# A new estimate of TensorE's times in the scheduler of a two-layer diffusion step: the same instructions in another order

## The chip, the cores and the metric

The kernel runs on one core of one Trainium2 chip, in one launch. The metric is the device time of that launch in microseconds (us). A core has TensorE (PE in the profile, with its weight loads as PEld), VectorE (DVE), ScalarE (ACT), GpSimd (POOL) and SyncE (SP), which here only issues transfers. Each engine works through its own instructions in program order, and waits where an operand is not there or a buffer is not free.

## The reference

A hybrid diffusion step of two layers on 1024 latent tokens and 256 context tokens, 1024 features wide, in float32. Layer 0 projects the tokens, runs a recurrence over them in both directions (RWKV-7, 8 heads of 64), runs a short gated convolution beside it, and projects back. Layer 1 is attention with 16 query heads and 4 key heads of 64. Cut to what matters here:

```
def rwkv_scan(S0, r, w, k, v, kk, a, reverse):
    def step(S, inp):
        r_t, w_t, k_t, v_t, kk_t, a_t = inp
        sk = jnp.einsum('bhvk,bhk->bhv', S, kk_t)
        S = (S * w_t[:, :, None, :] - sk[..., None] * (kk_t * a_t)[:, :, None, :]
             + v_t[..., None] * k_t[:, :, None, :])
        return S, jnp.einsum('bhvk,bhk->bhv', S, r_t)
    ...
def rwkv_conv_mixer(h, S0, w_in, ...):
    proj = h @ w_in
    ...
    S_f, y_f = rwkv_scan(S0[:, 0], ..., False)
    S_b, y_b = rwkv_scan(S0[:, 1], ..., True)
    ...
    out = jnp.concatenate([out_a, out_b], axis=-1) @ w_out
def block_attention(q, k, v):
    ...
        s = jnp.einsum('bqhgd,bhkd->bhgqk', qblk, k).astype(f32) * scale
        p = jax.nn.softmax(s, axis=-1).astype(v.dtype)
        return jnp.einsum('bhgqk,bhkd->bqhgd', p, v)
```

## The kernel before

**The work on TensorE.** The dense projection of layer 0 multiplies 34 slices of 128 columns of its weights with three blocks of tokens (512, 256, 512). Weights and activations are split into a high and a low half (`whi`, `wlo`, `h_hi`, `h_lo`), so that each of the eight tiles of a slice is a group of three products: `mm<-h_hi,whi`, `mm<-h_lo,whi`, `mm<-h_hi,wlo`. ScalarE makes `whi`, VectorE or GpSimd `wlo`. Counted as products of 512 columns the projection has 2040 of them. These are the filler: nothing waits for one of them for long.

**The scan.** The recurrence is worked off in 20 steps (five for each of four head pairs), each of four chunks of 64 tokens in both directions. A step is prepared (`iv<-lor,lw`, decays), then its token-token products are made (`interact`: `wk<-s,bk`, 32 instructions on 64x64 tiles of the array, of 128 columns each; `wk<-ident,bk` are transposes). The triangular inverse that a step needs goes out to DRAM (`n_d`), is solved on VectorE by some 62 small instructions (`acc`, `tmp`), and comes back over DRAM (`w_d`, `w`); `merge` completes it by three groups of sixteen 32x32 products (`iv<-ident,w`, `iv<-t,nn`, `iv<-w,zz`). Then comes the chain. For each chunk: `ch<-hv,s` (what u comes from), a copy to `xs`, `py<-s,hv`, `ch<-xs,w` (u), a copy into `hv` by ScalarE or VectorE, `ch<-hv,tbk` (the state), four VectorE instructions that make the next chunk's `hv`, and `py<-br,hv` (the rest of the output). A chunk starts when the one before it has given its state, and a chain when the chain before it has ended and its own inverse is there. After a chain the groups that both directions have passed are closed (`iv<-y,ones`, `iv<-sqy,ones`).

**After the scan** come the output projection of layer 0 (`mm<-wts,omh`), the projections of layer 1, attention (scores `py<-qa,ka` and `py<-qb,kb`, maxima from `mm<-ka,qa`, weighted sums `pv<-pe,v_sb` on 128x64 tiles) and the last projection.

**What sets the order.** Nothing of the order is written by hand. The class `Loom` (L112) holds some fifty generators in the order of `PRECEDENCE`; each says before what it issues next which engine and operands it begins with. `run` (L320) takes the first generator whose next piece could start at most a little after TensorE's estimated time (`LEAD` and a number of its own), and otherwise the one that could start first. `when` (L307) works out that start from `clock[engine]` and from the estimated ends of what wrote and read the operands. Each issued instruction moves these estimates on (`issued`, L241). For VectorE, ScalarE, GpSimd and transfers the estimate is a table of cost per instruction and element. For TensorE it is L251 to L261: 0.107 us for a transpose; else columns / 2400 MHz, times four for float32; and, for a product with at most 64 weight columns that follows one to other columns of the output, 0.053 us, after which the next counts in full again. `paced` (L224) doubles that when the estimated use of the array in a stretch was low. TensorE's estimated clock is then the end of the product. A wrong estimate costs nothing by itself; it changes which piece is taken next on every engine.

Of the kernel before, what the change touches and what calls it, by code (L numbers as in the profile page):

```python
# [10 lines left out]
F32R = mybir.dt.float32r  # L11
# [6 lines left out]
P = 128  # L18
D = 1024
KT = D // P  # L20
NS = 1024
# [3 lines left out]
# their order: the weights of a slice arrive during the first and go during the last  # L25
BLOCKS = (0, 2, 1)
# [11 lines left out]
# us per instruction and per element of a partition; what an engine must be ahead to be chosen  # L38
# [3 lines left out]
# the clock of the tensor engine goes by its use in windows of so many us  # L42
WINDOW = 3.413

# functions of the scalar engine whose tables displace each other
# [12 lines left out]
class Ring:  # L58
    """n buffers; take() holds the one that is free first until it is released"""
# [17 lines left out]
    def free(self):  # L77
        """when the buffers are free that nobody holds: (time, number)"""
        held = set(self.busy.values())
        return sorted((max((r[6] + 0.1 for r in self.loom.log.get(self.places[k][1], ())), default=0.0), k)  # L80
                      for k in range(self.n) if k not in held)
# [7 lines left out]
    def move(self, k, other):  # L89
        """buffer k, which is free, to another ring"""  # L90
# [8 lines left out]
    def ready(self, m):  # L99
        """when m are free, or None"""  # L100
# [4 lines left out]
class Into:  # L105
    """an operand that is written"""
# [5 lines left out]
class Loom:  # L112
    """Fixes the order of the instructions of every engine. Generators yield before what they issue
    next: the engine and operands that it begins with (buffers to come as their ring), or a condition.
    By an estimate of the engines' times the first generator goes on that would not hold up its engine."""

    def __init__(self, tc):
# [8 lines left out]
        self.last = None  # L126
# [36 lines left out]
    def region(ap):  # L163
        if ap.space == DRAM:
            # rows and columns
# [25 lines left out]
    def item(self, ap, write):  # L191
        """an operand: its buffer, region, whether it is in a bank, which serves one engine at a time"""
        return [self.slot.get(ap.tensor.name, ap.tensor.name), *self.region(ap), ap.space == PSUM, write, -1, None]

    def free(self, e, item):
        """when engine e can read or write an operand"""
# [27 lines left out]
    def paced(self, start, dur, rows):  # L224
        """how long a matrix product takes at the clock that the use of the array has earned"""
# [8 lines left out]
        while left > 0:  # L234
            part = min(left, w - start)
            self.use[w] = self.use.get(w, 0.0) + part * (rows // 32) / 4
            left -= part
            start, w = w, w + WINDOW
        return dur

    def issued(self, e, name, a, k, r):  # L241
# [9 lines left out]
        if e == "T":  # L251
            group = None
            if name == "transpose":
                dur = 0.107
            else:
                dur = max(0.054, n * (1 if ins[0].dtype == F32R else 4) / 2400.0)
                if ins[0].free_size() <= 64:
                    group = outs[0].start_partition() if callable(outs[0].start_partition) else outs[0].start_partition
                    if self.last is not None and group != self.last:
                        dur, group = 0.053, None  # L260
            self.last = group  # L261
# [15 lines left out]
        if e == "T":  # L277
            dur = self.paced(start, dur, ins[0].partition_size())
        if e == "D":
# [11 lines left out]
    def pick(self, engines, n, *aps, bias="V"):  # L291
        """the one of the engines that is done first with n elements per partition"""
# [4 lines left out]
    def needed(self, need):  # L297
        """engines, operands, rings with how many of them, how much ahead of others that are late"""
# [8 lines left out]
    def when(self, need):  # L307
        """when what a generator begins with could start, or None"""
# [11 lines left out]
    def run(self, gens):  # L320
        """the generators, in the order of their precedence, with what each may be late"""
# [4 lines left out]
        self.window, self.use, self.slow = WINDOW, {}, False  # L326
        self.moved = 0.0
        self.on = True
        while self.live:
# [12 lines left out]
            # what its engine can do before that  # L342
# [15 lines left out]
def hybrid_step(  # L358
# [26 lines left out]
    # constants that depend on shapes alone  # L385
# [1934 lines left out]
```

## Time and profile before

| | us |
|---|---|
| median of 3 runs (2295.11 to 2309.25) | 2300.24 |
| span of the profiled execution | 2307.4 |
| TensorE busy in it | 2118.9 |
| VectorE busy in it | 1574.4 |
| ScalarE, GpSimd busy in it | 1147.3, 988.8 |

The profiled execution lies within the range of the runs and a little over their median. Every record of a helper has the same line (L140 before, L141 in the changed kernel), so groups are told apart by the names out<-in. In a row on time, "idle before" is how long the engine stood still just before the instruction and what released it. A float32 product leaves two records, a float32r product and a transpose one, so four products `ch<-hv,tbk` are eight records.

### The profile page before, as it was taken

The numbers are of one execution on the slowest core, as the hardware profiler recorded it, in microseconds if no ns is written. First come the engines' busy times: TensorE is split into PE (matmuls) and PEld (weight loads), VectorE is DVE, ScalarE is ACT, GpSimd is POOL, SyncE is SP. The second block draws the span as 40 slices with busy tenths as digits, with TensorE's granted clock in tenths as the row PEclk, the third lists the DMA queues.
The fourth block names the chain that finished last, engine by engine and source line by source line (L and its number), as shares of the span: only waits on it lengthen the run. The fifth ranks groups of instructions, "written<-read, shape, count | busy, mean of one in ns | idle before, by whom it ended". The sixth has DMA issues, their size and how long they took to land.

```text
span 2307.4 us, 41359 instructions
## 1 busy us (share of the span) xinstructions
PE 2118.9 (92%) x14602; PEld 1431.2 (62%) x14602; DVE 1574.4 (68%) x3499; ACT 1147.3 (50%) x2644; POOL 988.8 (43%) x1126
## 2 busy tenths in 40 slices
PE   4998888899989999899789999999999999999998
PEld 1486666666656666666567788876444444444487
DVE  3346888768887877776656635546887888788543
ACT  3446656555555546553345623233655556555422
POOL 2434443334343533442233412312577666766822
PEclk7999999899988989998799999999999999999999
DMA  7834434333443343332356523222101110010233
GB/s 277 290 101 119 116 100 116 89 86 90 116 118 88 78 118 87 95 76 65 119 169 202 163 87 95 87 94 88 35 25 38 31 33 25 26 31 19 82 124 105
DMA packets 325172, 225.12 MB, mean 98 GB/s; under 512 B 164402, under 2 KB 279268, under 8 KB 322916
## 3 DMA queue, kind: packets, MB, share of 16 engines
q1 hardware_dynamic: 324964, 222.47, 32.6%
q8 instruction: 115, 1.88, 0.3%
q14 instruction: 93, 0.76, 0.1%
HBM read 159.79 MB, written 57.28 MB: 94 GB/s over the span
## 4 chain that ended last, share of the span: by engine, by line
PE 40%; DVE 9%; issue 3%; DMA 3%; ACT 2%; POOL 1%; SPq 0%; DVEq 0%; POOLq 0%; ACTq 0%
PE mm L140 24%; PE pv L140 6%; PE wk L140 5%; PE py L140 5%; DVE zs L140 2%; DVE mx L140 2%; DVE rz L140 1%; ACT pe L140 1%; PE ch L140 1%; DVE tmp L140 1%; DVE acc L140 1%; DMA om<-om_d 1%; SPq L140 0%; PE iv L140 0%; POOL zs L140 0%
## 5 line engine op out<-in xcount | busy, mean ns | idle before, releaser
L140 POOL TENSOR_TENSOR zs<-zs,pe 128x512 f32<-128x512 f32 x241 | 323.4, 1361 | 120.2 <-ACT pe L140 116.8
L140 PE MATMUL mm<-h_hi,whi 128*128 128x512 f32 (+1 forms) x816 | 336.8, 413 | 4.7 <-ACT whi L140 4.5
L140 DVE TENSOR_REDUCE mx<-mm 128x1 f32<-128x512 f32 (+1 forms) x416 | 267.6, 665 | 67.8 <-PE mm L140 64.7
L140 PE MATMUL mm<-h_hi,wlo 128*128 128x512 f32 (+1 forms) x816 | 301.2, 369 | 12.5 <-DVE wlo L140 11.5
L140 PE MATMUL mm<-h_lo,whi 128*128 128x512 f32 (+1 forms) x816 | 299.1, 367 | 0.0
L140 PE MATMUL mm<-wts,omh 128*128 128x512 f32 x960 | 239.8, 405 | 7.8 <-ACT wts L140 4.5
L140 ACT ACTIVATE pe<-py 128x512 f32<-128x512 f32 (+1 forms) x278 | 155.8, 579 | 140.7 <-PE py L140 125.3
L140 POOL TENSOR_TENSOR wlo<-wraw,whi 128x128 fp32r<-128x128 f32 x228 | 111.6, 495 | 242.4 <-ACT whi L140 198.4
L140 PEld LDWEIGHTS mm<-wts,omh 128*128 128x128 f32 x960 | 181.8, 193 | 53.1 <-ACT wts L140 5.7
L140 PE MATMUL pv<-pe,v_sb 128*64 128x512 f32 (+1 forms) x832 | 212.0, 598 | 2.1 <-DVE rz L140 1.8
L140 PEld LDWEIGHTS mm<-h_hi,whi 128*128 128x128 f32 x816 | 159.2, 195 | 50.5 <-issue 13.4
L140 PEld LDWEIGHTS mm<-h_hi,wlo 128*128 128x128 f32 x816 | 160.1, 196 | 42.1 <-DVE wlo L140 15.0
L140 DVE TENSOR_TENSOR acc<-acc,tmp 128x60 f32<-128x60 f32 (+23 forms) x620 | 168.8, 274 | 20.8 <-issue 2.9
L140 PE MATMUL mm<-ka,qa 128*128 128x512 f32 (+1 forms) x416 | 168.5, 435 | 10.5 <-DVE mx L140 7.7
L140 PEld LDWEIGHTS mm<-h_lo,whi 128*128 128x128 f32 x816 | 160.5, 197 | 14.6
L140 PE MATMUL mm<-wts,h_hi 128*128 128x512 f32 x480 | 151.2, 396 | 0.0
L140 POOL TENSOR_TENSOR hg<-hv,gc 64x128 f32<-64x128 f32 x152 | 65.2, 429 | 193.3 <-DVE hv L140 180.3
L140 PEld LDWEIGHTS mm<-ka,qa 128*128 128x128 f32 x416 | 73.4, 187 | 119.0 <-DVE mx L140 78.9
L140 ACT ACTIVATE whi<-wraw 128x128 fp32r<-128x128 f32 x272 | 80.3, 305 | 81.3 <-PE mm L140 37.8
L140 DVE SCALAR_TENSOR_TENSOR hv<-ch,gc,hg 64x64 f32<-64x64 f32 x288 | 81.3, 282 | 56.5 <-PE ch L140 49.7
L140 PE MATMUL py<-qa,ka 128*128 128x512 f32 (+1 forms) x278 | 114.6, 413 | 0.7 <-ACT pe L140 0.5
L140 PE MATMUL mm<-h_hi,wts 128*128 128x512 f32 (+1 forms) x384 | 111.7, 361 | 0.8 <-DVE mx L140 0.2
(248 smaller groups left out, 4410.1 us busy)
## 6 DMA issues: line engine op xcount, KB each, us to landing
wraw<-in_w_in_e_dram SPq DMA_DIRECT2D x272, 64.0 KB
wada<-in_w_ada_dram SPq DMA_DIRECT2D x16, 1024.0 KB
inp<-rkv_d SPq DMA_DIRECT2D x40, 384.0 KB
om<-om_d SPq DMA_DIRECT2D x52, 256.0 KB
wraw<-in_w_in_o_dram SPq DMA_DIRECT2D x40, 256.0 KB
wada<-in_w_ada_dram SPq DMA_DIRECT2D x16, 512.0 KB
rkv_d<-nb SPq DMA_DIRECT2D x24, 256.0 KB
lor<-lora_d SPq DMA_DIRECT2D x40, 128.0 KB
```

The source lines that it names most:

```text
L140: r = f(*a, **k)
```

## The change

The estimate for TensorE moves into a method of its own, `product`. It knows the size of the tile of the array that a product takes (`tiling`: rows and columns in units of 32) and which of the 16 parts it covers. A product of another tile size than the last starts 0.094 us after all before it have drained and takes longer by the loading of its weights; one of the same tile size starts when its own parts are free. Products on different parts overlap, and after a product that does not cover the whole array TensorE's clock is 0.014 us after its start. `paced` gets the share of the array that is in use and not yet counted, and a float32 product counts 1.68 ns a column, a float32r product 0.455, a transpose 0.84. The rest of the difference takes comments away.

```
-        self.last = None
+        self.tiling, self.parts, self.drained = None, {}, 0.0
...
-    def paced(self, start, dur, rows):
+    def paced(self, start, dur, share):
...
-            self.use[w] = self.use.get(w, 0.0) + part * (rows // 32) / 4
+            self.use[w] = self.use.get(w, 0.0) + part * share
...
+    def product(self, name, start, ins, out):
+        at = lambda x: (x.start_partition() if callable(x.start_partition) else x.start_partition) // 32
+        k, m = ins[0].partition_size(), ins[0].free_size()
+        tiling = tuple(next(x for x in (1, 2, 4) if n <= 32 * x) for n in (k, m))
+        parts = [(i, j) for i in range(at(ins[0]), at(ins[0]) + tiling[0]) for j in range(at(out), at(out) + tiling[1])]
+        n = out.free_size()
+        dur = n * (0.84e-3 if name == "transpose" else 0.455e-3 if ins[0].dtype == F32R else 1.68e-3)
+        dur = max(dur, 0.05)
+        if tiling != self.tiling:
+            start = max(start, self.drained + 0.094)
+            dur += 32 * tiling[1] / 1200.0
+            self.tiling = tiling
+        else:
+            start = max([start] + [self.parts.get(x, 0.0) for x in parts])
+        share = tiling[0] / 4 * max(0.0, start + dur - max(start, self.drained)) / dur
+        end = start + self.paced(start, dur, share)
+        for x in parts:
+            self.parts[x] = end
+        self.drained = max(self.drained, end)
+        self.clock["T"] = end if len(parts) == 16 else start + 0.014
+        return start, end
...
-            group = None
-            if name == "transpose":
-                dur = 0.107
-            else:
-                dur = max(0.054, n * (1 if ins[0].dtype == F32R else 4) / 2400.0)
-                if ins[0].free_size() <= 64:
-                    group = outs[0].start_partition() if callable(outs[0].start_partition) else outs[0].start_partition
-                    if self.last is not None and group != self.last:
-                        dur, group = 0.053, None
-            self.last = group
+            dur = 0.0
...
-            dur = self.paced(start, dur, ins[0].partition_size())
-        if e == "D":
+            start, end = self.product(name, start, ins, outs[0])
+        elif e == "D":
```

The program has the same products, copies and transfers; their order differs on every engine. Two places on TensorE show it. The first is the chain of the scan's seventh step, from the products that make u in its second chunk to the third chunk; before, it stood like this (`ch` is the chain's bank, `wk` and `iv` those of the steps to come):

```order
L140 MATMUL ch_6400<-xs,w_194 64x64 x4
L140 MATMUL wk_6535<-kds,ones_80 128x256
L140 MATMUL iv_6541<-lor,lw_3669 128x256 x2
L140 MATMUL ch_6400<-hv,tbk 64x64 x4
L140 MATMUL wk_6550<-s_6224,bk 64x128 x2
L140 MATMUL wk_6551<-s_6224,bk 64x128 x2
L140 MATMUL py_6510<-br,hv 64x64 x2
L140 MATMUL py_6511<-br,hv 64x64 x2
L140 MATMUL wk_6550<-s_6224,bk 64x128 x2
L140 MATMUL wk_6551<-s_6224,bk 64x128 x2
L140 MATMUL ch_6400<-hv,s_4691 64x64
```

In the changed kernel the same stretch, from the state's products to the next chunk, is this (`mm` is a bank of the dense projection):

```order
L141 MATMUL ch_6451<-hv,tbk 64x64 x4
L141 MATMUL mm_6436<-h_hi,whi 128x512
L141 MATMUL mm_6436<-h_lo,whi 128x512
L141 MATMUL mm_6436<-h_hi,wlo 128x512
L141 MATMUL py_6545<-br,hv 64x64 x2
L141 MATMUL py_6546<-br,hv 64x64 x2
L141 MATMUL mm_6436<-h_hi,whi 128x512
L141 MATMUL mm_6436<-h_lo,whi 128x512
L141 MATMUL mm_6436<-h_hi,wlo 128x512
L141 MATMUL ch_6451<-hv,s_4985 64x64
```

The token-token products of the step to come have left the gap, and two groups of dense products stand in it. The second place is the end of the scan on TensorE, where the last step's inverse is merged. Before, the dense projection was already used up there, and what stood between were the closing of the step before (`iv<-y`, `iv<-sqy`), gates of the next stage (`dg`) and its first products (`omh`):

```order
L140 MATMUL wk_14108<-dg_14091,ones 128x512
L140 MATMUL wk_14138<-dg_14121,ones 128x512
L140 MATMUL iv_14160<-y,ones_80 128x256
L140 MATMUL mm_14163<-wts_14147,omh_14142 128x512
L140 MATMUL mm_14163<-wts_14148,omh_14142 128x512
L140 MATMUL mm_14163<-wts_14147,omh_14143 128x512
L140 MATMUL mm_14163<-wts_14151,omh_14142 128x512
L140 MATMUL mm_14163<-wts_14152,omh_14142 128x512
L140 MATMUL mm_14163<-wts_14151,omh_14143 128x512
L140 MATMUL iv_14173<-sqy,ones_80 128x256
L140 MATMUL iv_14178<-ident,w_195 32x32 x16
L140 MATMUL iv_14210<-t_14195,nn 32x32 x16
```

In the changed kernel the same merge begins here:

```order
L141 MATMUL mm_14059<-h_hi,whi 128x512
L141 MATMUL mm_14059<-h_lo,whi 128x512
L141 MATMUL mm_14059<-h_hi,wlo 128x512
L141 MATMUL iv_14065<-ident,w_195 32x32 x16
L141 MATMUL mm_14059<-h_hi,whi 128x512
L141 MATMUL mm_14059<-h_lo,whi 128x512
L141 MATMUL mm_14059<-h_hi,wlo 128x512
L141 MATMUL mm_14059<-h_hi,whi 128x512
L141 MATMUL mm_14059<-h_lo,whi 128x512
L141 MATMUL mm_14059<-h_hi,wlo 128x512
L141 MATMUL iv_14094<-t_14082,nn 32x32 x16
```

The last merge now lies among the last dense products, ahead of the next stage's.

## Rows read from the trace of the kernel before

**Rows 1.** The page: the span, and TensorE's busy time, its share and instructions.
```profile
span 2307.4 us, 41359 instructions
PE 2118.9 (92%) x14602; PEld 1431.2 (62%) x14602; DVE 1574.4 (68%) x3499; ACT 1147.3 (50%) x2644; POOL 988.8 (43%) x1126
```

**Rows 2.** Stretches: length, busy us per engine (instructions), clock, DMA share, GB/s.
```profile
62.00:268.00 206.00, 186.71 (x1117) 132.64 (x1116) 113.90 (x243) 107.79 (x241) 81.80 (x121) 0.98 0.51 161
268.00:1117.00 849.00, 766.25 (x8263) 564.19 (x8263) 662.63 (x1972) 464.38 (x1245) 327.67 (x551) 0.94 0.36 93
1117.00:1176.00 59.00, 41.55 (x351) 25.01 (x346) 34.66 (x85) 23.48 (x54) 14.05 (x18) 0.77 0.52 159
...
1599.00:2188.00 589.00, 569.89 (x2367) 277.89 (x2365) 469.41 (x619) 334.94 (x646) 405.60 (x306) 1.00 0.13 38
```

**Rows 3.** Waits of TensorE's products, 268 to 1176 us: total, times, longest.
```profile
PE ch L140 <- DVE hv L140: 18.8, 29, 2.9
PE mm L140 <- DVE wlo L140: 11.5, 4, 3.7
PE ch L140 <- ACT hv L140: 7.0, 19, 1.5
...
PE iv L140 <- DVE y L140: 4.9, 5, 2.3
```

**Rows 4.** Waits of TensorE's weight loads, same stretch.
```profile
PEld ch L140 <- DVE hv L140: 30.8, 43, 3.2
...
PEld ch L140 <- ACT hv L140: 17.9, 37, 1.9
```

**Rows 5.** TensorE in time, a chain's second chunk: start, us, what [idle before].
```profile
558.64 0.45 PE L140 MATMUL ch<-hv,tbk 128*64 128x64 f32 x8
559.02 0.45 PE L140 MATMUL wk<-s,bk 64*64 64x128 f32 x8
559.29 0.34 PE L140 MATMUL py<-br,hv 64*64 64x64 f32 x6
...
560.52 0.45 PE L140 MATMUL ch<-hv,s 128*64 128x64 f32 x8 [0.62 <-DVE hv L140]
```

**Rows 6.** TensorE in time, two chunks of the last chain.
```profile
1153.69 0.97 PE L140 MATMUL mm<-wts,omh 128*128 128x512 f32 x3
1154.59 0.45 PE L140 MATMUL ch<-hv,tbk 128*64 128x64 f32 x8
...
1158.66 1.66 PE L140 MATMUL mm<-wts,omh 128*128 128x512 f32 x6
1160.25 0.45 PE L140 MATMUL ch<-hv,tbk 128*64 128x64 f32 x8
1160.63 0.45 PE L140 MATMUL py<-br,hv 64*64 64x64 f32 x8
1162.05 0.45 PE L140 MATMUL ch<-hv,s 128*64 128x64 f32 x8 [0.97 <-DVE hv L140]
```

**Rows 7.** TensorE in time, the end of the scan.
```profile
1116.04 0.40 PE L140 MATMUL mm<-h_hi,wlo 128*128 128x512 f32 x1
...
1132.37 0.69 PE L140 MATMUL iv<-ident,w 32*32 32x32 f32 x32 [0.56 <-ACT sqy L140]
...
1144.64 0.70 PE L140 MATMUL ch<-hv,s 128*64 128x64 f32 x8
...
1167.64 0.70 PE L140 MATMUL iv<-y,ones 128*128 128x256 f32 x2 [1.36 <-DVE y L140]
...
1175.79 0.51 PE L140 MATMUL mm<-wts,omh 128*128 128x512 f32 x1
```

**Rows 8.** `wk<-s,bk`: first and last start; one step's last, and its merge, in time.
```profile
L140 PE MATMUL wk<-s,bk x1280: 269/269/473, 183.5 to 1067.9; 64*64 64x128 f32 x183
...
521.25 0.39 PE L140 MATMUL wk<-s,bk 64*64 64x128 f32 x6
...
572.72 0.69 PE L140 MATMUL iv<-ident,w 32*32 32x32 f32 x32
```

More of the change, by code (lines that the diff above doesn't have):

```diff
@@ L326, in run @@
         self.window, self.use, self.slow = WINDOW, {}, False
+        self.tiling, self.parts, self.drained = None, {}, 0.0
         self.moved = 0.0
@@ L826, in hybrid_step @@
     class Step:
+        pass
     def make_steps():
```

## Prediction

> **What bounds the kernel now.** I read the stretches first, then who waited for whom on TensorE, then the order of single visits in time. TensorE is busy for 92% of the 2307.4 us span [rows 1], and the stretches differ [rows 2]: while attention runs it is busy 569.89 of 589 us at the full clock, so there only its own work counts; during the scan (268 to 1117 us) it is busy 766.25 of 849 us, at 0.94 of the clock; from 1117 to 1176 us, when the scan's last steps run and the dense products are used up, only 41.55 of 59 us, at 0.77. What can be won lies in the scan and its end. The waits name what ends TensorE's idle time there [rows 3]: 18.8 us at 29 places for `hv` from VectorE (the new state of a chunk), 7.0 us at 19 places for `hv` from ScalarE (u, copied out of its bank), 11.5 us at 4 places for the low half of a split weight. The weight loads, which run ahead of the products, stood longer for the same two: 30.8 and 17.9 us [rows 4].
>
> One such wait in time [rows 5]: the products `ch<-hv,tbk` start at 558.64, the next chunk's `ch<-hv,s` at 560.52, and TensorE stood idle for 0.62 us of these 1.88 us. In between stand eight instructions `wk<-s,bk` and the four `py<-br,hv`. The old estimate takes such a product as 0.213 us, and as 0.053 us if the one before it went to the other half of the columns; eight are 1.07 us by it. In the rows the first four start at 559.02 and what follows them at 559.29: 0.27 us, since four 64x64 tiles run side by side. So the scheduler believed the gap filled when it was not. At 1160.25 only `py<-br,hv` stands in between, and the next chunk starts 1.80 us later with 0.97 us idle [rows 6].
>
> **The change, part by part.** No instruction is added or removed; durations on every engine stay, and only the order moves. I counted over TensorE's whole order, before and now.
>
> *Cover of the chain.* Of 60 places where a chunk's `ch<-hv,tbk` is followed by the next chunk of its step, 23 had no dense product in between and 9 have none now; of the 76 places from `ch<-xs,w` to `ch<-hv,tbk` it was 33 and is 13. Three dense products that stand alone among small tiles last 0.90 us (1153.69 to 1154.59 [rows 6]). With one such group before `py<-br,hv` and one behind it, 0.38 + 0.90 + 0.38 + 0.90 = 2.56 us cover the 1.88; with one group 1.66 us leave 0.2. I scale the waits by the places that stay bare: 18.8 x 14/23 = 11.4 and 7.0 x 20/33 = 4.2 go, **15.6 us** in all. Bounds: nothing, if the states are late because VectorE is late; 30.8 x 14/23 + 17.9 x 20/33 = 29.6 us, if what the weight loads waited counts. I take the idle time of the products, which is time that nothing else filled.
>
> *The end of the scan.* Before, the last dense product starts at 1116.04, the last step's merge (`iv<-ident,w`) at 1132.37, its chain at 1144.64, its closing at 1167.64, and the products of the next stage run on from 1175.79 [rows 7]: 59.75 us. Now the merge's three groups stand among dense products, and the dense products end one visit after that chain has begun. What is left is the chain (1144.64 to 1167.64, 23.00 us) and the closing (to 1175.79, 8.15 us), 31.15 us. TensorE's work that moves out of this end is still to be done: three merge groups of 0.69 us each (2.1 us), 27 products `mm<-wts,omh` fewer before the end (54 stood there, 27 do now) at 0.23 us (6.2), three visits of the chain before at 0.38 (1.1) and four single products that I put at 1 us together: 10.4 us. The end gains 59.75 - 31.15 - 10.4 = **18.2 us**. Bounds: nothing, if TensorE waits for the inverse ahead of the merge instead; 28.6 us, if the moved work fits into waits. I take the middle sum, because the dense products between the last step's `wk<-s,bk` and its merge are 129 now and were 108, and the 64 us there (to 1132.37 from 1067.9 [rows 7, 8]) hold waits of the closing before it.
>
> *Switches between tile sizes.* TensorE's order has 1389 places where the tile size changes, and had 1312; 849 became 906 in the scan, 442 became 466 in attention. Six dense products among small tiles last 1.59 us (1158.66 to 1160.25), three last 0.90 [rows 6]: three more cost 0.69, 0.23 each, so the group of three pays 0.21 us for two switches, 0.105 each. 77 more cost **8.1 us**. Bounds: nothing, where TensorE waits anyway, and 8.1; I count them all. The Trainium skill (TensorEngine Tiling (Array Packing), Key Properties) says that changing the tiling mode, not just the tile, drains the TensorE; that speaks against this change, and the rows agree that a switch costs. The skill gives no price there; from the fixed part of a single product's latency that it states for the full clock (TensorE: Matmul & The Clock Gate, Single matmul latency: 398 cycles, 0.166 us) an estimate is 77 x 0.166 = 12.8 us, and with it the predicted time would be 4.7 us longer.
>
> *The scan's first chunk.* 606 dense products (counted as 512 columns) stand ahead of it, and 537 did: 69 x 0.23 = 15.9 us of work moves forward. I cost this at nothing: from 62 to 268 us TensorE was idle for 206 - 186.71 = 19.3 us [rows 2], which can take it, and the 2040 dense products are the same in sum. If it is not taken there, the scan begins up to 15.9 us later.
>
> *The rest.* The waits for split weights (11.5 us) and for the closing of a group (4.9 us for `y` from VectorE, [rows 3]) stay, some elsewhere; I count no change. Attention has the same products and exponentials between the same buffers; SyncE's queue carries the same transfers and moves with the rest.
>
> Sum: -15.6 - 18.2 + 8.1 = -25.7 us, 2307.4 to 2281.7 us. The profiled execution is 7.2 us over the median of 2300.2 us; by the same difference the median becomes **2274.5 us**.
>
> **The rivals.**
>
> *The inverse is late.* Between a step's `wk<-s,bk` and its merge lies the inverse, made by VectorE through two trips over DRAM. Before, the fewest dense products there were 93, once, in 51.5 us (521.25 to 572.72 [rows 8]); all others had 102 or more. Now five steps have 93 to 99. If VectorE keeps its pace, TensorE waits ahead of these merges, and ahead of the last one. For: with fewer waits the same products pass faster. Against: TensorE did not stand idle before the 93. Priced at 2 us for each of five (between 4.9/5 = 1 and the 3.7 of the longest wait for a weight, [rows 3]), and without the gain of the end: -15.6 + 8.1 + 10 = +2.5, 2303 us.
>
> *The chains get longer (slower).* The products that cover the waits stand inside the chains: 612 dense products there, 540 before. A chain's chunks follow each other, and a chain the one before it. If the pauses between chains are set by the inverse and do not shrink, 72 x 0.23 = 16.6 us and the later first chunk's 15.9 us lengthen the scan, and the gains are the chain waits alone: 16.6 + 15.9 - 15.6 + 8.1 = +25.0, 2325 us. It decides once the pauses keep more than about 25 of the 32.5 us. Against it: the dense products between the chains fell from 1002 to 837, so that work is not there to lengthen the pauses.
>
> *More than costed.* The weight loads' figures are the right ones, the moved work fits into waits, and switches lie in waits: -29.6 - 28.6 = -58.2, 2242 us at the most, and some 2255 for a part of it.
>
> *Nothing reaches the time.* VectorE, busy 662.63 of 849 us [rows 2], gives its results when it did before; the waits change their names, 2300 us.
>
> **How the numbers follow.** The forecast holds 0.50 (its own range 2260 to 2290), more than costed 0.17, the late inverse 0.15, nothing 0.07, longer chains 0.11. A measurement of this kernel can tell about 1% from no change, here 2277 to 2323 us. Of the forecast some six tenths lie under 2277 (0.30), which with the larger gain makes 0.47 faster; the rest of it, the late inverse and nothing make 0.42 the same; longer chains 0.11. The range goes from the full gain, 2242, to 2306, a little beyond the late inverse; it leaves out the longer chains and little else.
>
> **What would show it.** In the new profile between 268 us and the end of the scan: TensorE's wait for `hv` from VectorE near 7 us at about 11 places, from ScalarE near 3; from the last dense product to the run of next-stage products about 31 us instead of 59.75; attention within 5 us of its 589 us. The forecast is wrong if the merges show waits for the inverse, if the first chunk starts later than 268 us by 16 and the scan keeps its length, or if waits for split weights grow.

## The result and the profile after

The changed kernel is slower: 2381.8 us (2375.7 to 2382.2) beside 2297.7 (2289.6 to 2309.2) for the kernel before, a ratio of 1.035 with a 95% interval of 1.032 to 1.039. The prediction was 2274.5 us; 2381.8 lies outside its range, and the sign is wrong.

The page of the changed kernel, span and engines, answers [rows 1]: 73 us more of span, 40 of them in which TensorE counts as busy.

```profile
span 2380.2 us, 41309 instructions
PE 2159.4 (91%) x14602; PEld 1436.0 (60%) x14602; DVE 1534.5 (64%) x3506; ACT 1145.5 (48%) x2634; POOL 994.9 (42%) x1135
```

Its stretches, cut at the same products as [rows 2] (columns as there): up to the scan's first chunk, from there to the last dense product, to the end of the scan, the output projection of layer 0, and attention.

```profile
62.00:293.00 231.00, 205.15 (x1228) 147.07 (x1230) 130.84 (x285) 115.97 (x263) 91.81 (x137) 0.98 0.49 152
293.00:1151.00 858.00, 765.64 (x8275) 553.60 (x8270) 650.01 (x1982) 466.04 (x1238) 304.13 (x520) 0.93 0.35 90
1151.00:1189.00 38.00, 27.77 (x198) 16.42 (x196) 21.84 (x50) 16.23 (x35) 9.90 (x13) 0.70 0.48 152
1189.00:1334.00 145.00, 124.45 (x521) 96.45 (x520) 73.36 (x145) 71.07 (x161) 54.61 (x39) 0.91 0.54 172
1652.00:2263.00 611.00, 589.45 (x2363) 278.25 (x2362) 433.52 (x605) 326.06 (x631) 432.81 (x335) 0.99 0.13 37
```

The stretch ahead of the first chunk is 25 us longer, the next 9, the end of the scan 21 shorter (38 for 59). So the scan ends 13 us later than before, at 1189 for 1176. Then the output projection takes 145 us where it took 116 (1176 to 1291), layer 1's projections 318 for 308, attention 611 for 589: 29, 10 and 22 us more. The last projection takes 3 less. That is the 73 us.

The waits of TensorE's products in the scan (293 to 1189 us) answer [rows 3]:

```profile
PE ch L141 <- DVE hv L141: 24.9, 23, 2.6
PE mm L141 <- DVE wlo L141: 20.6, 8, 3.7
PE ch L141 <- ACT hv L141: 6.0, 5, 2.0
PE iv L141 <- DVE y L141: 5.5, 9, 1.0
```

and those of its weight loads [rows 4]:

```profile
PEld ch L141 <- DVE hv L141: 36.8, 34, 2.8
...
PEld ch L141 <- ACT hv L141: 17.8, 30, 2.1
```

The waits of the chain stand at fewer places, 28 for 48, and are longer in sum, 30.9 us for 25.8.

### The profile page after: what moved, and what is told of

The parts are those of the page before. It is cut to its first block, busy times and chain, and to the rows that moved or that the text cites. A ratio compares the mean times of both kernels' runs of the same rounds, so it can differ in the third digit from the quotient of the medians.

```text
span 2380.2 us, 41309 instructions
## 1 busy us (share of the span) xinstructions
PE 2159.4 (91%) x14602; PEld 1436.0 (60%) x14602; DVE 1534.5 (64%) x3506; ACT 1145.5 (48%) x2634; POOL 994.9 (42%) x1135
## 5 line engine op out<-in xcount | busy, mean ns | idle before, releaser
L141 POOL TENSOR_TENSOR zs<-zs,pe 128x512 f32<-128x512 f32 x274 | 354.8, 1315 | 110.2 <-ACT pe L141 99.8
L141 PE MATMUL mm<-h_hi,whi 128*128 128x512 f32 (+1 forms) x816 | 345.3, 423 | 5.9 <-ACT whi L141 5.7
L141 DVE TENSOR_REDUCE mx<-mm 128x1 f32<-128x512 f32 (+1 forms) x416 | 262.1, 665 | 113.4 <-PE mm L141 110.3
L141 POOL TENSOR_TENSOR wlo<-wraw,whi 128x128 fp32r<-128x128 f32 x209 | 101.4, 491 | 271.0 <-ACT whi L141 214.8
L141 PE MATMUL mm<-ka,qa 128*128 128x512 f32 (+1 forms) x416 | 162.8, 431 | 11.0 <-DVE mx L141 6.5
L141 DVE TENSOR_TENSOR acc<-acc,tmp 128x60 f32<-128x60 f32 (+24 forms) x620 | 161.3, 262 | 17.6 <-DVE tmp L141 0.7
L141 PE MATMUL py<-qa,ka 128*128 128x512 f32 (+1 forms) x278 | 120.9, 436 | 0.0
L141 ACT ACTIVATE pe<-wk 128x512 f32<-128x512 f32 (+1 forms) x138 | 80.2, 581 | 78.6 <-PE wk L141 75.4
```

What stands on the lines that cost most here:

```text
L141: r = f(*a, **k)
```

## The experiments

**How they are read.** All stages are cut at the same products in each trace: *first chunk* is the start of the first `ch<-hv,s`; *dense end* the start of the last product of the dense projection; *next stage* the first `mm<-wts,omh`; *its end* the end of the output projection; the projections of layer 1 run from there to the first score `py<-qa,ka`, attention from there to its last `pv<-pe,v_sb`. Times are us from the span's start, ratios go to the kernel before. Beside a measured time some expectations name the planner's own new estimate: the new method run along over a finished order without choosing anything in it. It is a number of the program and no time. For the order before it gives 2106, for the changed one 2165.

| kernel | ratio | first chunk | dense end | next stage | its end | projections of layer 1 | attention |
|---|---|---|---|---|---|---|---|
| before | 1 | 268 | 1116 | 1128 | 1291 | 307.5 | 588.5 |
| changed | 1.035 | 293 | 1151 | 1168 | 1334 | 317.8 | 610.8 |
| e1 new in attention | 1.005 | 268 | 1103 | 1116 | 1277 | 307.5 | 598.6 |
| e2 new till scan's end | 1.017 | 295 | 1150 | 1166 | 1323 | 307.5 | 591.1 |
| e3 new numbers, old rules | 1.034 | 289 | 1141 | 1159 | 1322 | 317.8 | 622.5 |
| e4 new rules, old numbers | 1.018 | 271 | 1123 | 1136 | 1315 | 307.8 | 605.6 |
| e5 float32r 0.455 alone | 1.051 | 288 | 1176 | 1188 | 1348 | 317.5 | 624.7 |
| e6 float32r 0.425 alone | 1.024 | 291 | 1168 | 1180 | 1334 | 315.0 | 594.3 |
| e7 float32r 0.400 alone | 1.004 | 295 | 1083 | 1122 | 1282 | 317.9 | 590.5 |
| e8 weights later | 1.005 | 273 | 1112 | 1137 | 1296 | 307.5 | 589.5 |
| e9 float32r 0.465 alone | 1.033 | 298 | 1141 | 1156 | 1318 | 315.7 | 617.4 |
| e10 float32 1.68 alone | 0.999 | 270 | 1106 | 1123 | 1286 | 307.6 | 583.6 |
| e11 new rules, numbers lower | 1.009 | 275 | 1110 | 1136 | 1294 | 313.3 | 583.3 |
| e12 best by the estimate | 1.021 | 300 | 1136 | 1176 | 1334 | 307.5 | 587.9 |
| e13 scatter of 1% | 1.019 | 300 | 1144 | 1158 | 1317 | 307.5 | 593.5 |
| e14 the same, other phase | 1.011 | 283 | 1121 | 1144 | 1307 | 307.5 | 586.9 |
| e15 scatter of 0.1% | 1.008 | 267 | 1119 | 1133 | 1290 | 307.6 | 588.3 |
| e16 float32r 0.455 in attention | 1.017 | 269 | 1107 | 1120 | 1282 | 307.5 | 624.8 |

**Which stage pays for what.** Two kernels change over from one estimate to the other at a fixed place, so that up to it the order is word for word that of the one kernel. In e1 it is where attention's memory is opened:

```
...
 moved.add("attention")
+loom.new, loom.clock["T"] = True, max(loom.clock["T"], loom.drained)
```

> The old estimate up to the point where attention's memory is opened, the new one from there on; so the order of the first 8277 of TensorE's 10658 products, and of what stands before that on every engine, is that of the kernel before, word for word. Theory A (each stage pays for the estimate under which it was ordered): the stages up to 1599 us take what they took, attention takes about 611 us where it took 588, the whole is 2298 + 22 = 2320 us, ratio 1.010. Rival (attention in the changed kernel only inherits what the scan and the projections left it: buffers, keys and queries in another state): attention 588, 2298 us, ratio 1.000. Planner's own new estimate, run along over the finished order: attention 573 for the order before, 615 for the changed one, 601 for this one.

2312.7 us, ratio 1.0046 (1.002 to 1.007). Attention took 598.6 us, between the two expectations (611 and 588): 10 of the 22 us belong to the order made there. In e2 the new estimate rules up to the scan's end and the old one behind it (`loom.new = False` where `loom.lead = LEAD[1]` stands):

> The new estimate up to the end of the scan (the place where the memory of layer 1 is opened), the old one from there on; TensorE's first 6424 products stand as in the changed kernel. Theory A: the scan ends at 1189 us as in the changed kernel. If the output projection behind it waits for its weights, whose loading begins only when the dense products are used up, it ends near 1334 us in whatever order (145 us where the kernel before took 116), and then projections and attention take the 308 and 588 us of the kernel before: 2298 + 43 = 2341 us, ratio 1.019. Rival (the 29 us more of the output projection come from its own order): it takes 116 us, 2298 + 13 = 2311 us, ratio 1.006. Planner's own new estimate over the finished order: 130 and 109 us for the output projection in the changed kernel and before, 129 here; 2118 in all, 2106 for the order before, 2165 for the changed one.

2340.4 us, ratio 1.0165 (1.013 to 1.020): theory A. The projections and attention are back at 307.5 and 591 us. The output projection, though ordered by the old estimate, took 136 us and not 116: it inherits most of its loss from the scan, 20 of the 29 us.

**Rules or numbers.** The change has two parts, new rules (tiles, switches, the clock 14 ns after the start of a small tile) and new costs per column. Each alone:

```
e3:  ...
     -                dur = max(0.054, n * (1 if ins[0].dtype == F32R else 4) / 2400.0)
     +                dur = max(0.054, n * (0.455e-3 if ins[0].dtype == F32R else 1.68e-3))
e4:  -        dur = n * (0.84e-3 if name == "transpose" else 0.455e-3 if ins[0].dtype == F32R else 1.68e-3)
     +        dur = 0.107 if name == "transpose" else n * (1 if ins[0].dtype == F32R else 4) / 2400.0
```

> The old rules for TensorE (no tiles, no switches, the clock at the end of each product) with the new numbers alone: 0.455 ns a column of a float32r product for 0.417, 1.68 for 1.667 of a float32 one, 0.84 of a transpose. Theory R (the rules do the harm: the switches, and TensorE's clock that goes on 14 ns after the start of a small tile): as before, 2298 us within 1%. Theory N (the numbers do it: a float32r product that counts 9% more shifts what looks late beside TensorE): slower like the changed kernel, 2360 to 2400 us, in the output projection, the projections of layer 1 and attention. Theory C (the kernel before is a lucky order among many, and any other number draws another): slower too, but with the loss at other places than the changed kernel's. Planner's own new estimate over this order: 2183, that is 77 more than over the order before; projection 137, attention 617.

> The new rules (tiles, switches, parts side by side, clock 14 ns after the start) with the old numbers (512 columns of float32r 0.213 us, a transpose 0.107, float32 1.667 ns a column). Theory R: slower like the changed kernel, 2360 to 2400 us. Theory N: as before, 2298 within 1%. Theory C: slower by 1 to 4%, neither like the one nor like the other. Planner's own new estimate over this order: 2133, 27 more than over the order before: scan 992 for 979, output projection 111, projections 309 as before, attention 597 for 573; by that some 2330 us.

e3 took 2382.2 us, ratio 1.034 (1.031 to 1.037), the time of the changed kernel with none of its rules. e4 took 2346.6, 1.018 (1.015 to 1.022). So the rules are not needed for the loss, and theory R falls as the whole cause. Which number it is:

> The kernel before with one number of its estimate changed: a float32r column counts 0.455 ns for 0.417, as in the changed kernel; rules, float32 and transposes as before. Theory N1 (this number is what does the harm in the run with the new numbers alone, since a dense product that counts 9% more makes other work look late beside TensorE): 2360 to 2400 us, ratio 1.03 to 1.04, with 590 to 606 dense products ahead of the first chunk and 318 us of projections. Rival (the 0.8% on the float32 products, of which the chain and attention consist): within 1% of before. Planner's own new estimate over this order: 2222, 116 more than over the order before; output projection 175, projections 323, attention 616.

> The kernel before with a float32 column at 1.68 ns for 1.667 in its estimate, 0.8% more; float32r, transposes and rules as before. If the float32r number is what harms: within 0.5% of before, 2295 to 2310 us. Theory C: slower by about 0.5 to 2% although the number hardly moved, 2311 to 2345 us. Planner's own new estimate over this order: 2118 (2106 over the order before): scan 991 for 979, output projection 103 for 109, attention 578 for 573.

e5 (0.455 for 0.417 ns a float32r column, nothing else) took 2418.5 us, 1.051 (1.048 to 1.054), above the expected 2360 to 2400 and more than the changed kernel itself. e10 (1.68 for 1.667 ns a float32 column) took 2299.0, 0.999 (0.997 to 1.001), with a scan in another order (1289 switches of the tile size in all for 1312): theory C had put it higher and is wrong there, not every other order loses.

**Is it the value of that number?** If it were, the loss should grow with it.

> The kernel before with a float32r column at 0.425 ns for 0.417 in its estimate, 2% more; nothing else. Theory N (the harm grows with the number): a fifth of the way to 0.455, so +0.7%, 2318 us. Theory C (the order before was kept because it happened to be fast; any other number draws another order, and these lie 1 to 4% higher whichever way the number goes): 2325 to 2395 us. Planner's own new estimate over this order: 2172, 66 more than over the order before, nearly all of it in the output projection (166 for 109).

> The kernel before with a float32r column at 0.400 ns for 0.417 in its estimate, 4% less; nothing else. Theory N (the harm grows with the number): as before or faster, 2280 to 2302 us. Theory C (any other number draws another order that lies 1 to 4% higher): 2325 to 2395 us. Planner's own new estimate over this order: 2133, 27 more than over the order before: scan 991 for 979, output projection 100 for 109, projections 323 for 309, attention 583 for 573.

> The kernel before with a float32r column at 0.465 ns for 0.417 in its estimate, more than in the changed kernel (0.455, which gave 2418 us alone). Theory N (the harm grows with the number; so far 0.400 gave 2309, 0.417 2300, 0.425 2357, 0.455 2418): 2418 us or more. Theory C (each number draws an order anew, and there is no law in the number): the planner's own new estimate over this order is 2173, 49 less than for 0.455 and like that for 0.425, so 2340 to 2375 us.

0.425 took 2357.3 us (1.024, 1.021 to 1.028), 0.400 took 2308.6 (1.004, 1.002 to 1.006), 0.465 took 2376.0 (1.033, 1.030 to 1.037), a microsecond above theory C's figures. A step of 2% costs half of what 9% costs, and 0.465 costs less than 0.455. So in the whole time there is no law in the number, and theory N is out in the form in which it stood; 0.400 fits neither theory's figures. Three kernels keep every mean and only scatter the old durations:

```
...
+            self.drawn += 1
+            dur *= 1 + 0.01 * math.sin(12.9898 * self.drawn + 1)
```

> The kernel before with its old estimate, each of TensorE's durations in it scattered by up to 1% of either sign (a sine of the product's number), so that the mean of every kind stays. Theory N (TensorE's mean pace in the estimate is what matters): within 0.5% of before, 2290 to 2313 us. Theory C (any other order of the scan lies higher; the order before was a favourable one): 1 to 3% slower, 2325 to 2370 us, lost up to the end of the output projection; projections 308 and attention 590 us within 6 us. Planner's own new estimate over this order: 2158 (2106 over the order before).

> The same scatter of 1% with another phase. Theory N: within 0.5% of before, 2290 to 2313 us. Theory C: 1 to 3% slower, 2325 to 2370 us, at other places of the scan than with the first phase. Planner's own new estimate over this order: 2136.

> The same scatter, a tenth of it: 0.1% of either sign. TensorE's first 1081 products stand as before. Theory N: within 0.5% of before. Theory C (the planner is chaotic, the size of the disturbance does not matter once one choice has flipped): 0.5 to 3% slower, 2312 to 2370 us. Planner's own new estimate over this order: 2126.

2339.9 us (1.019, 1.016 to 1.022), 2322.3 (1.011, 1.008 to 1.014) and 2315.6 (1.008, 1.005 to 1.011): all three slower, by under 2% but clear of no change, e14 in the gap between the two expectations, with the projections at 307.5 and attention at 587 to 594 us as before. A disturbance of a thousandth, which leaves TensorE's first 1081 products in place, costs 0.8%. In e13 and e14 the loss is there when the output projection ends, at 1317 and 1307 us, where it ends at 1277, 1282 and 1291 in the three executions with the order before; e15's profiled execution (span 2305.5) lies below its other runs and shows no place. This is theory C for the scan: other orders of it mostly lie higher, whatever made them other.

**Attention.** It was open whether its 22 us come with the number.

```
...
+        loom.column = 0.455e-3      (where attention's memory is opened; 1 / 2400 before)
```

> The kernel before up to the point where attention's memory is opened (the first 8282 of TensorE's products stand as before); from there on a float32r column counts 0.455 ns for 0.417 in the estimate, nothing else. If attention's loss belongs to that number there: 610 to 625 us for 588, the whole 2322 to 2338 us, ratio 1.009 to 1.016. If it is inherited from the scan and the projections: 588 to 592, ratio below 1.003. Planner's own new estimate over this order: attention 616 for 573.

2334.3 us, 1.0167 (1.014 to 1.020), attention 624.8 us behind an unchanged order: it does come with the number there, and even more so under the old rules. What differs in e16 is to be seen in the weight loads that wait for the bank of the maxima, `mm`, which VectorE empties (`mx`). The waits of weight loads in attention, before (1599 to 2187 us):

```profile
PEld mm L140 <- DVE mx L140: 74.6, 112, 1.6
```

and in e16 (1589 to 2214 us):

```profile
PEld mm L140 <- DVE mx L140: 111.0, 216, 1.5
```

TensorE in time shows how. Before, the products `mm<-ka,qa` come one at a time among the scores `py`, `wk`:

```profile
1850.66 0.50 PE L140 MATMUL mm<-ka,qa 128*128 128x512 f32 x1
1851.00 0.40 PE L140 MATMUL py<-qa,ka 128*128 128x512 f32 x1
1851.23 0.40 PE L140 MATMUL py<-qb,kb 65*128 65x512 f32 x1
1851.47 0.40 PE L140 MATMUL mm<-ka,qa 128*128 128x512 f32 x1
```

In e16 they come in pairs:

```profile
1852.43 0.88 PE L140 MATMUL mm<-ka,qa 128*128 128x512 f32 x2
1853.24 1.08 PE L140 MATMUL pv<-pe,v_sb 128*64 128x512 f32 x4
1854.25 0.73 PE L140 MATMUL mm<-ka,qa 128*128 128x512 f32 x2
```

The changed kernel makes the same pairs, but this wait does not grow there (1652 to 2262 us):

```profile
PEld mm L141 <- DVE mx L141: 63.7, 132, 1.4
```

So the wait for the bank goes with e16's loss and does not explain the 22 us of the changed kernel. Of these, some 20 stand in time in which TensorE counts as busy (589.45 us for 569.89 in the stretches above), at a granted clock of 0.99 for 1.00 in the mean; the clock can make up some 6 of them, an estimate from 0.01 of 611 us.

**The end of the scan.** In e8 the kernel before hands the memory of the scan's activations over, with which the next stage's weights begin to load, only when the last chain has begun:

```
-        yield lambda: filled and not evacs and not norms and not mm_ps.busy and not nbs.busy
+        yield lambda: filled and begun and not evacs and not norms and not mm_ps.busy and not nbs.busy
...
```

> The kernel before, with one condition more: the memory of the scan's activations changes hands (and with it the next stage's weights begin to load) when the dense products are used up and the last chain has begun, not when they are used up. TensorE's first 6200 products, up to the last dense product at 1116 us, stand as before. Theory W (from the last dense product on the path is the next stage's material: weights loaded from DRAM, split by ScalarE and VectorE, then tokens through the first projection; so what the changed kernel gained in idle at the scan's end it lost in the output projection): the first weight is split at about 1145 + 11 = 1156 instead of 1127, the scan ends some 5 to 10 us earlier than 1176, and the output projection ends 20 to 29 us later than 1291: 2322 to 2331 us, ratio 1.009 to 1.013. Rival (the weights are there long before they are needed and the projection is bound by TensorE): within 6 us of before, ratio 1.000 to 1.003.

2312.7 us, 1.005 (1.002 to 1.008). TensorE in time, the last dense product, the start of the last chain and the next stage's first product:

```profile
1111.77 0.40 PE L140 MATMUL mm<-h_hi,wlo 128*128 128x512 f32 x1
...
1131.94 0.70 PE L140 MATMUL ch<-hv,s 128*64 128x64 f32 x8
...
1136.73 1.23 PE L140 MATMUL mm<-wts,omh 128*128 128x512 f32 x3 [0.20 <-ACT omh L140]
```

The next stage's first product comes 25.0 us after the last dense one, where it comes 12.1 to 12.5 after it in the three runs with the order before; the end of the output projection comes 184.2 us after it instead of 173.7 to 175.4 (174.6 in the mean). Of 12.7 us of delay 9.6 arrive. The mechanism is theory W's; the size I expected was too large, because the last chain began 20 us after the last dense product and not 29.

**Can the estimate pick a better order?**

> The changed kernel with three of its numbers a little lower: float32r 0.430 ns a column for 0.455, float32 1.660 for 1.680, drained 0.090 us for 0.094. It is the best of 24 such redraws of the new rules by the planner's own new estimate, which gives it 2115 (2165 for the changed kernel, 2106 for the order before; the 24 run from 2115 to 2231, mean 2152). Theory C: faster than the changed kernel by 40 to 70 us, 2310 to 2340 us, with nothing in the rules changed. Theory R (the rules themselves cost 1.5 to 2%, as the run with new rules and old numbers might say): 2340 us or more.

> The new estimate up to the end of the scan, with 0.434 ns for 0.455 a float32r column, 1.682 for 1.680 a float32 one and 0.109 us for 0.094 drained; the old estimate from there on. It is the best of 72 redraws (24 each of the old rules with other numbers, of the new rules, and of the new ones in the scan alone) by the planner's own new estimate, which gives it 2101: 5 less than the order before. If that estimate ranks orders as the chip does: 2285 to 2305 us. Theory C says that the order before is about the best of as many draws: within 1.5% of it, 2290 to 2335 us, and not faster by more than 0.5%.

e11 took 2319.2 us, 1.009 (1.006 to 1.011): the changed kernel with three numbers lowered by 1.2 to 5.5% gives back 63 of its 84 us, with every rule in force. e12 took 2348.7, 1.021 (1.019 to 1.024), outside both expectations: the order that the estimate likes best loses 43 us by the end of the output projection (1334 for 1291). (Its estimate changes over where the next stage's weights begin to load, somewhat ahead of the scan's end.) The estimate ranks what comes behind the scan: 309 us for projections of 307.5 before and 323 for 317.5 and 317.9 in e5 and e7, 573 and 615 for an attention of 588 and 611. Whole orders it ranks only roughly. Of the fifteen with a total on record, the six at 2158 or more lose 1.9 to 5.1%, the nine from 2101 to 2136 at most 2.1%; but among these nine the one that it likes best, e12, loses the most. No kernel beat the one before.

## Why the prediction was wrong

Of the 73 us of span, 43 have come together by the end of the output projection, and layer 1's projections and attention add 32; the last projection gives 3 back. The sum had gains in the scan and its end and a price for switches; it put the first chunk, the output projection, layer 1 and attention at nothing.

**Cover of the chain (-15.6 us): wrong.** The covers came as counted, but the waits did not go (25.8 us became 30.9). The step took the state's way over VectorE as fixed and looked at TensorE's order alone. Over 60 places, from the start of `ch<-hv,tbk` to the end of the last `hv` that follows it, it took 2.13 us in the mean before and 2.62 now; the four `hv` instructions themselves take 1.13 us in both, and the time that VectorE spends on other work in between rose from 41.2 to 65.0 us in sum. (The same order scatters less: 2.08 and 2.15 us in e1 and e16, which have the order before there, and 2.60 in e2, which has the new one.) One such place, VectorE in time, changed kernel:

```profile
333.76 0.22 DVE L141 TENSOR_TENSOR acc<-acc,tmp 128x63 f32<-128x63 f32 x1
334.02 0.22 DVE L141 TENSOR_TENSOR tmp<-acc,nra 128x60 f32<-128x60 f32 x1
...
336.13 0.23 DVE L141 TENSOR_TENSOR tmp<-acc,nra 128x64 f32<-128x64 f32 x1
336.39 0.23 DVE L141 TENSOR_TENSOR acc<-acc,tmp 128x64 f32<-128x64 f32 x1
336.65 1.18 DVE L141 SCALAR_TENSOR_TENSOR hv<-ch,gc,hg 64x64 f32<-64x64 f32 x4
```

and TensorE beside it:

```profile
333.52 0.45 PE L141 MATMUL ch<-hv,tbk 128*64 128x64 f32 x8
...
334.79 0.45 PE L141 MATMUL py<-br,hv 64*64 64x64 f32 x8
337.88 0.70 PE L141 MATMUL ch<-hv,s 128*64 128x64 f32 x8 [2.64 <-DVE hv L141]
```

The products of the state are through by 333.97. VectorE first does ten more instructions of an inverse, and TensorE, with a dense group in the gap, still waits 2.64 us. The prediction had this as the lower bound of the term ("if the states are late because VectorE is late") and did not look at VectorE's order. With the new rules alone (e4) the way takes 2.42 us and the other work 60.4 us; with the new numbers alone (e3) 2.23 and 44.9.

**The end of the scan (-18.2 us): right in direction where it looked, and given back.** The end shrank from 59.75 to 38 us, where the sum had left 31. But the next stage's material begins to load when the dense products are used up, and that moment came 35 us later. The changed kernel in time, to be read beside [rows 7]:

```profile
1151.12 0.40 PE L141 MATMUL mm<-h_hi,wlo 128*128 128x512 f32 x1
...
1167.78 1.65 PE L141 MATMUL mm<-wts,omh 128*128 128x512 f32 x3
...
1189.17 0.79 PE L141 MATMUL mm<-wts,omh 128*128 128x512 f32 x1
...
1197.25 3.23 PE L141 MATMUL mm<-wts,omh 128*128 128x512 f32 x6 [4.40 <-ACT wts L141]
```

The last dense product to the end of the output projection took 175 us before and takes 183 now. (In e2, with the old estimate behind the scan's end, it is 173: so about 35 of the 43 us come with the later last dense product, and 8 with the projection's own order.) TensorE is busy for as much of it, before

```profile
1116.00:1291.00 175.00, 152.59 (x849) 113.27 (x848) 103.64 (x220) 88.57 (x200) 58.52 (x48) 0.90 0.57 180
```

and now

```profile
1151.00:1334.00 183.00, 152.22 (x717) 112.86 (x716) 95.20 (x195) 87.29 (x195) 64.51 (x51) 0.87 0.53 168
```

The idle time that left the scan's end stands in the projection, where ScalarE, which makes the split weights, waits longer for the transfer. Its waits, before in the first and now in the second stretch:

```profile
ACT wts L140 <- DMA wraw<-in_w_out_e_dram: 7.1, 8, 2.6
```

```profile
ACT wts L141 <- DMA wraw<-in_w_out_e_dram: 16.3, 8, 6.1
```

In 17 of the 18 orders of the table the stretch from the next stage's first product to its end is 153 to 166 us (179 in e4). So what counts for the end is when that stage can begin, and e8 shows that a delay there arrives for the most part. The idle time that the prediction meant to remove covered these loads; the prediction looked for what hides an edit, not for what the idle time itself hides. What bounds the 153 to 166 us was not tried.

**The first chunk (costed at nothing): wrong.** It starts 25 us later (293.4 for 268.1). TensorE is busy 18.4 us longer ahead of it (205.15 for 186.71), so the 69 products were not taken in idle time; that idle time did not shrink either (25.9 us for 19.3). Later the stretch up to the last dense product has as much busy time as before (765.64 for 766.25) though 69 dense products (15.9 us by the prediction) have left it, and 92 us of idle for 83. The last merge, two closings and the start of the last chain have moved in; by the prediction's prices (2.1 us for a merge's three groups, 0.38 for a visit) that is a few us, so most of the 15.9 is not accounted for. The later start (25 us) and the longer stretch (10) are how the dense products came to end 35 us later. By the condition in the prediction ("If it is not taken there, the scan begins up to 15.9 us later") this was the sign to weigh more.

**Attention and layer 1 ("no change"): wrong**, 22 and 10 us. The argument was that products and buffers are the same. The order is not, and both stages follow the float32r number: the projections take 307.5 to 307.8 us in all eleven kernels in which it stands at 0.417 there (for the scattered ones in the mean), with either rules, and 313 to 318 in all seven others, above it or below; attention takes 598.6 to 624.8 us in the six with 0.455 or 0.465 there and 583 to 594 in the others, but for e4 (605.6), which has the new rules with the old number. In all six the maxima come in 159 to 172 pairs, in the twelve others in 70 to 121. That the pairs are the cause was not tried alone; in e1 there are 159 of them and attention is only 10 us longer, and the wait that they bring in e16 did not grow in the changed kernel.

**Switches (+8.1 us): not what decided.** e9 has 1223 switches and e5 1273, both fewer than the 1312 before, and both lose. The 0.1 us for one was not measured by itself.

**Split weights.** They did not stay at 11.5 us at 4 places, but became 20.6 at 8, as the prediction named for a sign of failure.

**The rivals.** The only slower one, longer chains, had the right sign and a later first chunk, not the mechanism: from the first chunk to the start of the last chain the scan got shorter (293 to 1150, 857 us, for 268 to 1145, 877). Its first half came true: from their first `ch<-hv,s` to the last product in their bank the twenty chains take 495 us in sum for 442. But the pauses between them shrank by more, to 390 us from 456, as the prediction had argued against this rival. The late inverse showed as well, but small. The waits of TensorE for it, before (268 to 1176 us) and now (293 to 1189 us):

```profile
PE iv L140 <- DMA w<-w_d: 1.8, 3, 1.0
```

```profile
PE iv L141 <- DMA w<-w_d: 5.4, 7, 1.3
```

Missing was the plain rival that any change of the estimate draws a new order, which can be worse however true the estimate is. Of 17 other orders tried here (e1, e8 and e16 share all or nearly all of the scan's order with the one before) none is faster by more than 0.1%, four lie within 0.5%, and 13 lose 0.8 to 5%. The numbers say that the order before is at the low end of such draws; they do not say how it came there. The new estimate did not help: by its own count, too, the order that it made is worse than the one before (2165 for 2106). What falls short is the choice piece by piece, not only the estimate behind it.

What stays open: why a larger number bunches the maxima in attention, what makes TensorE's busy time there longer in the changed kernel, and which of the scan's many places makes one order of it 40 us longer than another.

## What to carry to other kernels

Where a planner fixes the order, a change of its numbers draws a new order, and one timing of one draw says little about the change; disturb the numbers by a thousandth first and see how far the time moves, and expect an order at the low end of such draws to lose. Before a stall is counted as a gain, ask which transfers and preparations run under it and which event starts them: if the next stage waits for that event and not for the stall's end, the time comes back there. A wait filled on one engine is only filled if the engine that ends it does not take on work in the same gap, so read the order of both.

## What was not expected of the hardware

The same order takes different times in the scan. The kernel before and e1 have the same first 8277 products, and the last dense one started at 1116 in one profiled execution and at 1103 in the other (1107 in e16). In the stretch from 268 to 1103 us, the kernel before and then e1:

```profile
268.00:1103.00 835.00, 752.25 (x8119) 554.31 (x8119) 653.66 (x1935) 460.79 (x1234) 324.50 (x547) 0.94 0.36 94
```

```profile
268.00:1103.00 835.00, 754.65 (x8255) 556.83 (x8247) 661.60 (x1970) 462.44 (x1244) 326.68 (x551) 0.95 0.36 95
```

In the same 835 us e1 comes 136 records further, at a granted clock of 0.95 for 0.94. So differences of under 15 us in the scan of a single execution are not read here, and the stages behind it, which agree to 0.1 us where their order is the same (projections of 307.5 us in the kernel before, e1 and e16), are the better ground for small ones.
